# Second ConvGLU mixer in seven products: where and when the sums of its weights are loaded, and which banks its accumulators use

## The chip, the cores and the metric

One core of one Trainium2 chip runs the whole program. Its engines work side by side, each through its own list of instructions in order: TensorE (PE; PEld is its weight load), VectorE (DVE), ScalarE (ACT), GpSimd (POOL) and SyncE (SP), which here only issues DMA transfers. POOL issues transfers too: those that add what they bring to what lies at the destination ("accumulating" below). The metric is the time of one execution in device microseconds; lower is better.

## The reference, cut to what matters

A small diffusion backbone of two layers, 512 latent and 256 context tokens of width 1024, all in fp32. Layer 0 mixes tokens by attention, layer 1 by a bidirectional mLSTM. After each comes a mixer over channels, and the one of layer 1 is what is changed. It sees the 512 latent tokens only:

```
def conv_ffn(h, w_up, conv_w, conv_b, w_down):
    gate, val = jnp.split(jnp.dot(h, w_up), 2, axis=-1)      # h 512 x 1024, w_up 1024 x 5632
    return jnp.dot(jax.nn.silu(dwconv(gate, conv_w, conv_b)) * val, w_down)   # w_down 2816 x 1024
```

`dwconv` is a convolution of width 3 over tokens, per channel.

## The kernel before, in words

*The seven products.* The 2816 channels are walked in NF = 22 chunks of 128. For a chunk f the up projection is a 2 x 2 block product: two column blocks of weights (g for the gate, v for the value), each in two halves of the inner dimension (k 0 to 3, k 4 to 7), times two token halves of 256. The kernel computes it as Winograd's form of Strassen's scheme, with seven block products in place of eight. The token sides (B11, B21, B22, T1 to T4) are made once by `norm_seven`, which also does the norm. The weight sides are g itself (tile a, products 1 and 2), sums of halves of g and v (products 5, 6, 3 and 7), and the second half of v (tile d, product 4).

Every fp32 operand is split in a high part, rounded to TensorE's fp32r, and a low part, the rest: an ACT cast (L43) and a DVE subtract (L44) in `split`. A product of two operands is three matmuls, so one of the seven is 4 x 3 = 12 matmuls of 256 columns (L390).

*The sums.* They are made by DMA. `load(f)` (L404 to L415) issues, per chunk, from SP: tile a (L408, 512 KB), three plain copies of 256 KB into blocks 0, 1 and 2 of tile R (L411) and tile d (L413); and from POOL two accumulating transfers: v's first half into blocks 0 to 2 (L414), then g's first half into block 1 (L415). Block 3 is made by DVE from block 1 and the second half of a (L451, in p3). Blocks 0 and 1 are then split as "S12" for products 5 and 6, blocks 2 and 3 as "S34" for products 3 and 7. R and d have two buffers each.

*The loop.* Iteration f calls load(f+1), p1(f), p7(f-1), a down step, p2(f), p5(f), p6(f), p4(f-1), a down step, p3(f). A down step (L479 on) is one of eight output blocks of the down projection of a group of four chunks: 12 matmuls of 512 columns (L493) and a DVE addition into X (L495). Down steps begin in iteration 5. After p3 comes the convolution (L457 to L459), Silu (L461), and after p4 the products with the value half (L473, L474) and a split.

*Accumulators.* PSUM has eight banks of 512 fp32 per partition. Tag "S" gives two tiles of two banks each (`A`), and T, U, R, O are one bank each (`B`). Y takes product 1, then 6, then 7, then 4; between them u2 (L446) and v2 (L467) are read from the partial sum. Z takes product 2, and W product 5, then 3. Two chunks' Y share a tile of tag S, one bank each, so four Y exist. Z and W of a chunk are the two halves of one bank, T or U in turn; ACT copies Z out at L432 and W at L440.

*Around it.* Before the mixer stand the last part of the mLSTM (`odd`), the last two heads' share of the output projection (L1669), and `norm_seven` in two token halves. Tile R lies in pool "ffn1", which is opened after the norm, in places of "o1" (those two heads' inputs) and "nrm" before it.

*What sets the order.* The program is written in the order of these calls, but a planner (the Tile framework's) places each engine's instructions: it keeps a clock of its own for every instruction, and on an engine that is free it takes, of those that it holds for ready, the one that stands first in the program. An instruction can so come to stand far ahead of its place in the program; on the chip the engine then waits at it. A buffer is given to its next tile when the instructions that read the old one are over.

Of the kernel before, what the change touches and what calls it, by code (L numbers as in the profile page):

```python
# [32 lines left out]
class Kernel:  # L33
# [331 lines left out]
            nc.scalar.copy(B["T4"][0][:, a], g[:, b])  # L365
            low("T4", a, g[:, b], nc.vector)

    def ffn_seven(self, l, X, B, pool):

        nc, i = self.nc, self.i
        nt, n = NL, NL // 2
        cw, cb = self.fcw[l], self.fcb[l]  # L380
        neg = pool.tile([128, KD], F32, name="neg")
        nc.vector.tensor_scalar(neg, self.mod[l][:, 40:48, 0], -1.0, None, op0=MUL)
        ch, act = {}, {}
        ypair = None

        def prod(ps, w, x, first, last):
            m = 0
            for k in range(4):
                for a, b in ((w[0], x[0]), (w[1], x[0]), (w[0], x[1])):
                    nc.tensor.matmul(ps, a[:, k], b[:, k], start=first and m == 0, stop=last and m == 11,  # L390
                                     skip_group_check=True)
                    m += 1

        def pair(src, cols=KD):
            if cols == KD:
                hi, lo = self.wtile("wh", KD, 128, F32R), self.wtile("wl", KD, 128, F32R)
            else:
                hi, lo = [pool.tile([128, 4, 128], F32R, tag="d" + x, name="d" + x, bufs=1) for x in "hl"]
            self.split(hi, lo, src)
            return hi, lo  # L400

        part = lambda w, h: [x[:, 4 * h:4 * h + 4] for x in w]

        def load(f):  # L404
            c = ch[f] = {}
            g, v = i["wup"][l, f, 0], i["wup"][l, f, 1]
            c["a"] = self.wtile("wr", KD, 128, F32)
            nc.sync.dma_start(c["a"], g)  # L408
            R = c["R"] = pool.tile([128, 4, 4, 128], F32, tag="R", name="R", bufs=2)
            for j, src in enumerate((v[:, 4:8], v[:, 4:8], g[:, 0:4])):  # L410
                nc.sync.dma_start(R[:, j], src)  # L411
            c["d"] = pool.tile([128, 4, 128], F32, tag="d", name="d", bufs=2)
            nc.sync.dma_start(c["d"], v[:, 4:8])  # L413
            nc.gpsimd.dma_start(R[:, 0:3], v[:, 0:4].unsqueeze(1).to_broadcast([128, 3, 4, 128]), accum_op=ADD)  # L414
            nc.gpsimd.dma_start(R[:, 1], g[:, 0:4], accum_op=ADD)  # L415

        def p1(f):
            nonlocal ypair
            c = ch[f]
            if f % 2 == 0:  # L420
                ypair = self.A("Y")
            c["Y"] = ypair[:, 512 * (f % 2):512 * (f % 2) + n]
            c["A1"] = pair(c["a"])
            prod(c["Y"], part(c["A1"], 0), B["B11"], True, False)

        def p2(f):
            c = ch[f]
            zw = self.B("TU")
            c["W"], Z = zw[:, n:2 * n], zw[:, 0:n]
            prod(Z, part(c["A1"], 1), B["B21"], True, True)  # L430
            g = c["g"] = pool.tile([128, nt], F32, tag="g", name="g", bufs=2)
            nc.scalar.copy(g[:, 0:n], Z)  # L432
            nc.vector.tensor_tensor(g[:, 0:n], g[:, 0:n], c["Y"], op=ADD)

        def p5(f):
            c = ch[f]
            c["S12"] = pair(c["R"][:, 0:2].rearrange("p s k c -> p (s k) c"))
            prod(c["W"], part(c["S12"], 0), B["T1"], True, False)
            p = c["p5"] = pool.tile([128, n], F32, tag="p5", name="p5", bufs=2)
            nc.scalar.copy(p, c["W"])  # L440

        def p6(f):
            c = ch[f]
            prod(c["Y"], part(c["S12"], 1), B["T2"], False, False)
            u = c["u2"] = pool.tile([128, n], F32, tag="u2", name="u2", bufs=2)
            nc.scalar.copy(u, c["Y"])  # L446

        def p3(f):
            c = ch[f]
            R = c["R"]  # L450
            nc.vector.tensor_tensor(R[:, 3], R[:, 1], c["a"][:, 4:8], op=ADD)  # L451
            c["S34"] = pair(R[:, 2:4].rearrange("p s k c -> p (s k) c"))
            prod(c["W"], part(c["S34"], 1), B["B22"], False, True)
            g = c["g"]
            nc.vector.tensor_tensor(g[:, n:nt], c["u2"], c["W"], op=ADD)
            y = c["y"] = pool.tile([128, nt], F32, tag="y", name="y", bufs=2)
            nc.scalar.activation(y, g, AF.Identity, bias=cb[:, f:f + 1], scale=cw[:, 1, f:f + 1])  # L457
            nc.vector.scalar_tensor_tensor(y[:, 1:nt], g[:, 0:nt - 1], cw[:, 0, f:f + 1], y[:, 1:nt], op0=MUL, op1=ADD)
            nc.vector.scalar_tensor_tensor(y[:, 0:nt - 1], g[:, 1:nt], cw[:, 2, f:f + 1], y[:, 0:nt - 1],  # L459
                                           op0=MUL, op1=ADD)  # L460
            nc.scalar.activation(y, y, AF.Silu)  # L461

        def p7(f):
            c = ch[f]
            prod(c["Y"], part(c["S34"], 0), B["T3"], False, False)
            v = c["v2"] = pool.tile([128, n], F32, tag="v2", name="v2", bufs=2)
            nc.vector.tensor_tensor(v, c["p5"], c["Y"], op=ADD)  # L467

        def p4(f):
            c = ch[f]  # L470
            prod(c["Y"], pair(c["d"], 4), B["T4"], False, True)
            y = c["y"]
            nc.vector.tensor_tensor(y[:, 0:n], y[:, 0:n], c["Y"], op=MUL)  # L473
            nc.vector.tensor_tensor(y[:, n:nt], y[:, n:nt], c["v2"], op=MUL)  # L474
            x = act[f] = [pool.tile([128, nt], F32R, tag="a" + e, name="a" + e, bufs=8) for e in "hl"]
            self.split(*x, y)
            del ch[f]

        def down(fs):  # L479

            nf = len(fs)
            cols = min(512, 1024 // nf)
            for o in range(KD):
                if o * 128 % cols == 0:
                    w = self.weights(i["wdn"][l, fs[0]:fs[0] + nf, :, o * 128:o * 128 + cols].rearrange("f p c -> p f c"),
                                     nf, cols)
                off = o * 128 % cols
                ps = self.B("RO")
                m = 0
                for j, f in enumerate(fs):  # L490
                    wh, wl = w[j]
                    for x, y in ((wh, act[f][0]), (wl, act[f][0]), (wh, act[f][1])):
                        nc.tensor.matmul(ps, x[:, off:off + 128], y, start=m == 0, stop=m == 3 * nf - 1)  # L493
                        m += 1
                nc.vector.scalar_tensor_tensor(X[:, o], ps, neg[:, o:o + 1], X[:, o], op0=MUL, op1=ADD)  # L495
                if fs[-1] == NF - 1:
                    nc.sync.dma_start(self.out[:, o], X[:, o])
                yield

        groups = [list(range(f, min(f + 4, NF))) for f in range(0, NF, 4)]  # L500
        todo = []

        def go():
            while todo:
                if next(todo[0], 0) is None:
                    return
                todo.pop(0)

        load(0)
        for f in range(NF + 1):  # L510
            for fs in groups:
                if f == fs[-1] + 2:
                    todo.append(down(fs))
            if f + 1 < NF:
                load(f + 1)
            one, two = f < NF, f > 0
            if one:
                p1(f)
            if two:
                p7(f - 1)  # L520
            go()
            if one:
                p2(f)
                p5(f)
                p6(f)
            if two:
                p4(f - 1)
            go()
            if one:
                p3(f)  # L530
        todo.append(down(groups[-1]))
        while todo:
            go()


    def conv(self, y, ps, w, b, segs):
# [986 lines left out]
    def build(self):  # L1523
        tc, nc, i = self.tc, self.nc, self.i
        with ExitStack() as es:
# [130 lines left out]
                "p (j k t) -> p j k t", j=6, k=4)  # L1656
            B.update({nm: [z[:, 2 * j], z[:, 2 * j + 1]] for j, nm in enumerate(("T1", "T2", "T3"))})
            kept = {}
            with tc.tile_pool(name="o1", bufs=1, reuse_waits="tile") as OP, \
                    tc.tile_pool(name="nrm", bufs=1, reuse_waits="tile", side="right") as NP:  # L1660
                x = [post(h, OP, "RO") for h in (6, 7)]
                for half in range(2):
                    t = slice(256 * half, 256 * half + 256)
                    for o in range(KD):
# [6 lines left out]
                                m += 1  # L1671
                        self.xupd(1, 16, X, ps, o, 256 * half, 256, 0)
                    self.norm_seven(NP, X, 1, B, half, 256, kept)
            RP.release()


            with tc.tile_pool(name="ffn1", bufs=1, reuse_waits="tile") as FP:
                self.we = FP
                self.ffn_seven(1, X, B, FP)
                self.we = None  # L1680
            hp.release()
            HP.release()

# [103 lines left out]
```

## Time and profile before

| | us |
|---|---|
| median of 3 runs | 1864.92 (1861.98 to 1868.36) |
| profiled execution | 1872.47 |
| its span | 1870.6 |

| engine | busy us | share of the span |
|---|---|---|
| PE | 1698.6 | 91% |
| PEld | 1483.5 | 79% |
| DVE | 1332.0 | 71% |
| ACT | 811.5 | 43% |
| POOL | 314.0 | 17% |

The span runs from the first instruction to the last. Busy shares are means over stages with different limits; the second mixer is the last quarter of the span, from about 1380 us. In the chain of waits each piece is put down to what released the next one; "issue" is time for which the profile shows no releaser. In the tables of instructions, `R<-in_wup` means that tile R is written from the up weights.

### The profile page before, as it was taken

To read this page: it belongs to the slowest core of one execution; us is meant where nothing else is said; L and a number is where in the kernel's file an instruction comes from. 1 tells how busy PE (TensorE), PEld (TensorE's weight loads), DVE (VectorE), ACT (ScalarE), POOL (GpSimd) and SP (SyncE) were. 2 spreads that over 40 slices of the span, in tenths; PEclk is the share of its full clock that TensorE was granted. 3 is DMA by queue.
4 is the path that set the end of the run, shared out by engine and by line. 5 is a ranking of instruction groups with operands and counts; after the bars stand their busy time and mean duration, and the time that the engine had idled before them with its cause. 6 is when DMAs were issued, how large, how long until landed. Compare 5 with 4: busy or idle time off the path is not lost.

```text
span 1870.6 us, 27080 instructions
## 1 busy us (share of the span) xinstructions
PE 1698.6 (91%) x10222; PEld 1483.5 (79%) x10222; DVE 1332.0 (71%) x2475; ACT 811.5 (43%) x1514; POOL 314.0 (17%) x348
## 2 busy tenths in 40 slices
PE   7998899999999999999999899999955788888889
PEld 3787788888888888888888788888845787777777
DVE  7998989987875767767665777877884554555555
ACT  3337879882521312222232665555353343333332
POOL 0343554540200000000000311211041111001000
PEclk9999999999999999999999999999877898989889
DMA  8450000034343433444323411111227766555642
GB/s 295 130 160 15 11 7 18 1 137 145 114 157 102 147 113 124 136 124 136 102 91 102 125 57 46 46 57 55 93 72 171 180 158 159 139 147 152 154 109 82
DMA packets 94922, 204.15 MB, mean 109 GB/s; under 512 B 10052, under 2 KB 38724, under 8 KB 94408
## 3 DMA queue, kind: packets, MB, share of 16 engines
q1 hardware_dynamic: 82820, 179.34, 29.2%
q0 software_dynamic: 11968, 23.07, 7.3%
q8 instruction: 81, 1.33, 0.3%
q14 instruction: 49, 0.40, 0.1%
q10 hardware_dynamic: 4, 0.01, 0.0%
HBM read 198.19 MB, written 4.20 MB: 108 GB/s over the span
## 4 chain that ended last, share of the span: by engine, by line
PE 53%; DVE 17%; DMA 13%; issue 9%; ACT 7%; POOL 2%; SPq 0%; POOLq 0%; DVEq 0%; ACTq 0%
PE psS L88 18%; DMA R<-in_wup 12%; PE psU L88 4%; PE psT L588 3%; PE psU L588 3%; DVE wl L44 2%; PE psR L88 2%; PE psT L88 2%; DVE junk L141 2%; PE S L681 1%; PE psO L588 1%; PE psR L588 1%; PE psO L726 1%; PE psO L493 1%; PE psR L98 1%
## 5 line engine op out<-in xcount | busy, mean ns | idle before, releaser
L43 ACT CAST wh<-wr 128x1024 fp32r<-128x1024 f32 (+2 forms) x165 | 170.4, 1034 | 218.9 <-PE psO L588 113.0
L44 DVE TENSOR_TENSOR wl<-wr,wh 128x1024 fp32r<-128x1024 f32 (+2 forms) x165 | 201.1, 1219 | 36.9 <-ACT wh L43 34.7
L88 PE MATMUL psS<-hl,wh 128*128 128x512 f32 (+1 forms) x640 | 216.6, 339 | 1.1 <-POOL hl L297 1.1
L88 PE MATMUL psS<-hh,wh 128*128 128x512 f32 (+1 forms) x640 | 216.5, 339 | 0.4 <-ACT hh L293 0.4
L88 PE MATMUL psS<-hh,wl 128*128 128x512 f32 (+1 forms) x640 | 216.0, 338 | 0.0
L141 DVE CUSTOM_DVE_ANT_0 y<-ar,cb 128x1024 f32<-128x1024 f32 x112 | 136.4, 1218 | 0.4 <-DMA ar<-in_ada 0.4
L88 PEld LDWEIGHTS psS<-hl,wh 128*128 128x128 f32 x640 | 120.5, 188 | 16.4 <-POOL hl L297 2.1
L88 PEld LDWEIGHTS psS<-hh,wh 128*128 128x128 f32 x640 | 120.4, 188 | 15.1 <-ACT hh L293 0.9
L88 PEld LDWEIGHTS psS<-hh,wl 128*128 128x128 f32 x640 | 120.2, 188 | 14.4
L276 POOL TENSOR_TENSOR sa<-sa,sq 128x512 f32<-128x512 f32 (+1 forms) x12 | 13.5, 1124 | 590.2 <-ACT sq L275 590.2
L451 DVE TENSOR_TENSOR R<-R,wr 128x512 f32<-128x512 f32 x22 | 15.2, 691 | 126.9 <-issue 104.5
L692 POOL TENSOR_SCALAR p<-p,rs 128x768 f32<-128x768 f32 (+1 forms) x96 | 74.2, 780 | 113.4 <-DVE rs L691 70.0
L390 PE MATMUL Y<-Ts,wh 128*128 128x256 f32 x352 | 82.7, 316 | 8.4 <-DVE y L473 7.1
L141 DVE CUSTOM_DVE_ANT_0 junk<-ar,cb 128x1024 f32<-128x1024 f32 x64 | 82.0, 1281 | 0.4
L539 ACT ACTIVATE y<-psS,fcb,fcw 128x512 f32<-128x512 f32 (+1 forms) x40 | 24.7, 668 | 127.9 <-PE psS L88 127.9
L541 DVE SCALAR_TENSOR_TENSOR y<-psS,fcw,y 128x511 f32<-128x511 f32 (+1 forms) x40 | 24.5, 611 | 74.5 <-ACT y L539 74.5
L44 DVE TENSOR_TENSOR wl<-R,wh 128x1024 fp32r<-128x1024 f32 x44 | 53.7, 1221 | 33.0 <-ACT wh L43 32.9
L390 PEld LDWEIGHTS Y<-Ts,wh 128*128 128x128 f32 x352 | 68.6, 226 | 9.7 <-DVE y L473 7.3
L43 ACT CAST wh<-R 128x1024 fp32r<-128x1024 f32 x44 | 46.0, 1050 | 46.6 <-issue 19.2
L414 POOL DMA_DIRECT2D R<-in_wup x22 | 28.7, 1324 | 214.0 <-DMA R<-in_wup 190.9
L635 DVE SCALAR_TENSOR_TENSOR X<-psU,mod,X 128x512 f32<-128x512 f32 (+1 forms) x45 | 30.0, 666 | 45.9 <-PE psU L588 35.9
L684 DVE TENSOR_REDUCE nm<-S 128x1 f32<-128x768 f32 x64 | 60.1, 945 | 2.0 <-PE S L681 1.6
(791 smaller groups left out, 5578.9 us busy)
## 6 DMA issues: line engine op xcount, KB each, us to landing
ar<-in_ada SPq DMA_DIRECT2D x88, 512.0 KB, 3.7
wr<-in_wup SPq DMA_DIRECT2D x66, 512.0 KB, 3.8
wr<-in_wdn SPq DMA_DIRECT2D x44, 512.0 KB, 3.5
R<-in_wup SPq DMA_DIRECT2D x66, 256.0 KB, 3.5
R<-in_wup POOLq DMA_DIRECT2D x22, 768.0 KB, 7.3
d<-in_wup SPq DMA_DIRECT2D x22, 256.0 KB, 4.4
R<-in_wup POOLq DMA_DIRECT2D x22, 256.0 KB, 4.5
pr<-in_adak SPq DMA_DIRECT2D x8, 512.0 KB, 5.9
```

The lines of the kernel that those rows point to most:

```text
L43: nc.scalar.copy(hi, src)
L44: nc.vector.tensor_tensor(lo, src, f32(hi), op=SUB)
L88: nc.tensor.matmul(ps, a, b[:, k, x0:x0 + n], start=i == 0, stop=i == 3 * nk - 1)
L141: nc.vector.tensor_tensor_reduce(out, raw, self.cb[:, c], 1.0, 0.0, MUL, ADD, self.mraw[l][:, n, c:c + 1])
L390: nc.tensor.matmul(ps, a[:, k], b[:, k], start=first and m == 0, stop=last and m == 11, skip_group_check=True)
L414: nc.gpsimd.dma_start(R[:, 0:3], v[:, 0:4].unsqueeze(1).to_broadcast([128, 3, 4, 128]), accum_op=ADD)
L539: nc.scalar.activation(y[:, t0:t0 + n], p, AF.Identity, bias=b, scale=w[1])
L541: nc.vector.scalar_tensor_tensor(y[:, t0 + 1:t0 + n], p[:, 0:n - 1], w[0], y[:, t0 + 1:t0 + n], op0=MUL, op1=ADD)
L588: nc.tensor.matmul(ps[:, 0:n], x[:, off:off + 128], y[:, t0:t0 + n], start=m == 0, stop=m == 3 * len(fs) - 1)
L635: self.nc.vector.scalar_tensor_tensor(X[:, o, t0:t0 + n], ps[:, 0:n], self.mod[l][:, g0 + o, c:c + 1], X[:, o, t0:t0 + n], op0=MUL, op1=ADD)
L684: nc.vector.tensor_reduce(nm, s[:, 0:nk], axis=AX.X, op=MAX, negate=True)
L692: nc.gpsimd.tensor_scalar(p[:, 0:nk], p[:, 0:nk], r, 1.0, op0=MUL, op1=MUL)
```

## The change

Tile R becomes two tiles of two blocks, R12 and R34, in a pool "sums" of their own, which is opened before the output projection's last part. `load_sums(l, f)` issues their loads: two plain copies of v's second half (256 KB each) into R12, one accumulating transfer of v's first half into both blocks (512 KB), a plain copy of all of g (512 KB) into R34, g's first half accumulated into R12's second block (256 KB), v's first half accumulated into R34's first block (256 KB), and d. It is called for chunks 0 and 1 before the output projection, and for f+2 at the end of iteration f. `load(f)` loads tile a alone. The add of block 3 (before L451) moves to p5, after the split of S12, and reads R12's second block in place of tile a. p1 and p2 of chunks 0 and 1 are called ahead of the loop.

Y is now the first half of one bank, T or U in turn, so two Y exist; Z and W are a bank each of a tile of tag S. Pool "m1" (OT and other mLSTM tiles) is released before "nrm" is opened.

```diff
@@ ffn_seven
         def load(f):
-            c = ch[f] = {}
-            g, v = i["wup"][l, f, 0], i["wup"][l, f, 1]
+            c = ch[f]
             c["a"] = self.wtile("wr", KD, 128, F32)
-            nc.sync.dma_start(c["a"], g)
-            R = c["R"] = pool.tile([128, 4, 4, 128], F32, tag="R", name="R", bufs=2)
-            for j, src in enumerate((v[:, 4:8], v[:, 4:8], g[:, 0:4])):
-                nc.sync.dma_start(R[:, j], src)
-            c["d"] = pool.tile([128, 4, 128], F32, tag="d", name="d", bufs=2)
-            nc.sync.dma_start(c["d"], v[:, 4:8])
-            nc.gpsimd.dma_start(R[:, 0:3], v[:, 0:4].unsqueeze(1).to_broadcast([128, 3, 4, 128]), accum_op=ADD)
-            nc.gpsimd.dma_start(R[:, 1], g[:, 0:4], accum_op=ADD)
+            nc.sync.dma_start(c["a"], i["wup"][l, f, 0])

         def p1(f):
-            nonlocal ypair
             c = ch[f]
-            if f % 2 == 0:
-                ypair = self.A("Y")
-            c["Y"] = ypair[:, 512 * (f % 2):512 * (f % 2) + n]
+            c["Y"] = self.B("TU")[:, 0:n]
...
         def p2(f):
             c = ch[f]
-            zw = self.B("TU")
-            c["W"], Z = zw[:, n:2 * n], zw[:, 0:n]
+            zw = self.A("ZW")
+            c["W"], Z = zw[:, 512:512 + n], zw[:, 0:n]
...
         def p5(f):
-            c["S12"] = pair(c["R"][:, 0:2].rearrange("p s k c -> p (s k) c"))
+            c["S12"] = pair(c["R12"].rearrange("p s k c -> p (s k) c"))
+            nc.vector.tensor_tensor(c["R34"][:, 1], c["R34"][:, 1], c["R12"][:, 1], op=ADD)
...
         def p3(f):
-            R = c["R"]
-            nc.vector.tensor_tensor(R[:, 3], R[:, 1], c["a"][:, 4:8], op=ADD)
-            c["S34"] = pair(R[:, 2:4].rearrange("p s k c -> p (s k) c"))
+            c["S34"] = pair(c["R34"].rearrange("p s k c -> p (s k) c"))
...
         load(0)
+        load(1)
+        for f in (0, 1):
+            p1(f)
+            p2(f)
         for f in range(NF + 1):
...
-            if f + 1 < NF:
+            if 0 < f < NF - 1:
                 load(f + 1)
             one, two = f < NF, f > 0
-            if one:
+            if one and f > 1:
                 p1(f)
             if two:
                 p7(f - 1)
             go()
+            if one and f > 1:
+                p2(f)
             if one:
-                p2(f)
                 p5(f)
                 p6(f)
...
             if one:
                 p3(f)
+            if f + 2 < NF:
+                self.load_sums(l, f + 2, ch)
...
+    def load_sums(self, l, f, ch):
+        nc, pool = self.nc, self.sums
+        g, v = self.i["wup"][l, f, 0], self.i["wup"][l, f, 1]
+        c = ch[f] = {}
+        r12 = c["R12"] = pool.tile([128, 2, 4, 128], F32, tag="R12", name="R12", bufs=2)
+        r34 = c["R34"] = pool.tile([128, 2, 4, 128], F32, tag="R34", name="R34", bufs=2)
+        for j in range(2):
+            nc.sync.dma_start(r12[:, j], v[:, 4:8])
+        nc.gpsimd.dma_start(r12, v[:, 0:4].unsqueeze(1).to_broadcast([128, 2, 4, 128]), accum_op=ADD)
+        nc.sync.dma_start(r34.rearrange("p s k c -> p (s k) c"), g)
+        nc.gpsimd.dma_start(r12[:, 1], g[:, 0:4], accum_op=ADD)
+        nc.gpsimd.dma_start(r34[:, 0], v[:, 0:4], accum_op=ADD)
+        c["d"] = pool.tile([128, 4, 128], F32, tag="d", name="d", bufs=2)
+        nc.sync.dma_start(c["d"], v[:, 4:8])
@@ build
-            with tc.tile_pool(name="o1", bufs=1, reuse_waits="tile") as OP, \
-                    tc.tile_pool(name="nrm", bufs=1, reuse_waits="tile", side="right") as NP:
-                x = [post(h, OP, "RO") for h in (6, 7)]
+            self.sums = tc.alloc_tile_pool(name="sums", bufs=1, reuse_waits="tile")
+            ch = {}
+            for f in range(2):
+                self.load_sums(1, f, ch)
+            OP = tc.alloc_tile_pool(name="o1", bufs=1, reuse_waits="tile")
+            x = [post(h, OP, "RO") for h in (6, 7)]
+            RP.release()
+            with tc.tile_pool(name="nrm", bufs=1, reuse_waits="tile", side="right") as NP:
...
-            RP.release()
+            OP.release()
```

## Rows read from the trace of the kernel before

**Rows 1.** The chain that ended last, of the whole span, by engine and line.

```profile
PE psS L88 18%; DMA R<-in_wup 12%; PE psU L88 4%; PE psT L588 3%; PE psU L588 3%; DVE wl L44 2%; PE psR L88 2%; PE psT L88 2%; DVE junk L141 2%; PE S L681 1%; PE psO L588 1%; PE psR L588 1%; PE psO L726 1%; PE psO L493 1%; PE psR L98 1%
```

**Rows 2.** Busy us by stage: PE, PEld, DVE, ACT, POOL; granted clock, DMA share, GB/s.

```profile
1380.00:1400.00 20.00, 4.34 (x30) 4.12 (x28) 17.82 (x34) 11.14 (x25) 12.08 (x8) 0.67 0.08 20
...
1440.00:1500.00 60.00, 46.60 (x322) 43.93 (x321) 34.29 (x52) 24.63 (x39) 8.70 (x8) 0.89 0.73 177
1500.00:1600.00 100.00, 84.26 (x520) 76.95 (x519) 52.77 (x77) 35.36 (x52) 9.61 (x9) 0.90 0.60 152
```

**Rows 3.** The chain in time order, one period and a sum before: start, us, what.

```profile
1558.72 8.80 DMA R<-in_wup
...
1572.19 0.69 DVE R L451
...
1576.67 3.52 DMA R<-in_wup
...
1580.77 6.63 DMA R<-in_wup
1587.40 4.98 issue
```

**Rows 4.** DVE's timeline in that period: start, us, line, operation, idle before.

```profile
1574.58 1.22 DVE L44 TENSOR_TENSOR wl<-R,wh 128x1024 fp32r<-128x1024 f32 x1
...
1581.42 1.22 DVE L44 TENSOR_TENSOR wl<-R,wh 128x1024 fp32r<-128x1024 f32 x1 [3.17 <-ACT wh L43]
...
1592.38 0.69 DVE L451 TENSOR_TENSOR R<-R,wr 128x512 f32<-128x512 f32 x1 [5.95 <-issue]
...
1594.65 1.22 DVE L44 TENSOR_TENSOR wl<-R,wh 128x1024 fp32r<-128x1024 f32 x1
```

**Rows 5.** Tile R, line 451: count, ns min/median/max, first and last start.

```profile
L451 DVE TENSOR_TENSOR R<-R,wr x22: 683/691/694, 1411.0 to 1806.6; 128x512 f32<-128x512 f32 x22
```

**Rows 6.** SP's timeline in that period.

```profile
1575.82 1.28 SPq L411 DMA_DIRECT2D R<-in_wup  x3
```

**Rows 7.** POOL's timeline in that period.

```profile
1580.77 1.28 POOL L414 DMA_DIRECT2D R<-in_wup  x1 [12.06 <-DMA R<-in_wup]
1587.69 0.90 POOL L415 DMA_DIRECT2D R<-in_wup  x1 [5.64 <-DMA R<-in_wup]
```

**Rows 8.** The chain near the end: a down step and the last product 3.

```profile
1816.43 2.80 PE psO L493 x12
...
1834.81 1.42 PE psU L390 x12
```

**Rows 9.** PE's timeline where product 1 of chunk 5 starts.

```profile
1484.65 0.28 PE L390 MATMUL Y<-B11h,wh 128*128 128x256 f32 x1
```

**Rows 10.** DMA from 1500 to 1800: queues, and one load with its landing.

```profile
q1 hardware_dynamic: 17616, 29.63, 29.8%
q0 software_dynamic: 7778, 15.01, 29.5%
...
wr<-in_wup SPq DMA_DIRECT2D x14, 512.0 KB, 4.2
```

**Rows 11.** Who waited for whom, 1500 to 1800: us in total, times, longest.

```profile
PE Y L390 <- DVE v L467: 25.9, 7, 5.3
...
PE psU L390 <- ACT g L432: 17.5, 7, 3.2
```

**Rows 12.** POOL's timeline around the norm.

```profile
1361.23 1.14 POOL L318 TENSOR_TENSOR sa<-sa,sq 128x256 f32<-128x256 f32 x1 [38.33 <-ACT sq L317]
...
1397.08 2.80 POOL L414 DMA_DIRECT2D R<-in_wup  x2
```

**Rows 13.** PE's timeline: the last matmul that reads V.

```profile
1340.07 0.27 PE L1478 MATMUL num<-V,Dh 128*128 128x130 f32 x1
```

**Rows 14.** DVE's timeline: the last gate, and T2's second low part.

```profile
1353.93 0.68 DVE L1520 SCALAR_TENSOR_TENSOR OT<-gt,psT 128x512 f32<-128x512 f32 x1
...
1398.81 0.68 DVE L359 SCALAR_TENSOR_TENSOR Ts<-h,Ts 128x512 fp32r<-128x512 f32 x1
```

More of the change, by code (lines that the diff above doesn't have):

```diff
@@ L366, in norm_seven, with ffn_seven @@
             low("T4", a, g[:, b], nc.vector)
-    def ffn_seven(self, l, X, B, pool):
+    def ffn_seven(self, l, X, B, pool, ch):
         nc, i = self.nc, self.i
@@ L382, in ffn_seven @@
         nc.vector.tensor_scalar(neg, self.mod[l][:, 40:48, 0], -1.0, None, op0=MUL)
-        ch, act = {}, {}
-        ypair = None
+        act = {}
         def prod(ps, w, x, first, last):
@@ L1673, in build @@
                     self.norm_seven(NP, X, 1, B, half, 256, kept)
-            RP.release()
+            OP.release()
             with tc.tile_pool(name="ffn1", bufs=1, reuse_waits="tile") as FP:
                 self.we = FP
-                self.ffn_seven(1, X, B, FP)
+                self.ffn_seven(1, X, B, FP, ch)
                 self.we = None
+            self.sums.release()
             hp.release()
```

## The prediction

> **What bounds the kernel now.** I read the chain of waits first. Loads into tile R have 12% of it, more than any line but the biggest of TensorE's [rows 1], and R exists in the second FFN alone. The table by stage says the same: TensorE is busy for 4.3 of 20 us from 1380, for 46.6 of 60 from 1440, and from 1500 on for a steady 84 of 100 at a granted clock of 0.90 [rows 2]. So the last 490 us have two troubles: a poor start (1380 to 1500) and a steady state that TensorE doesn't set.
>
> The chain of the steady state repeats one period [rows 3]: L451 at 1572.19, plain load of R, first accumulating load, a wait of 4.98 called "issue", and L451 again at 1592.38 [rows 4]. That is 20.2 us; all 22 calls lie between 1411.0 and 1806.6 [rows 5], 18.8 apart in the mean, as the first ones, with no down projection beside them, come faster.
>
> Why is R, with two buffers, loaded once per period in a closed loop? The DVE's order shows it [rows 4]. Of the two low splits of R in a period, the one at 1574.58 is S34 of chunk c, the one at 1581.42 is S12 of chunk c+1. L451 of chunk c+2 stands on DVE at 1592.38, AHEAD of S34 of chunk c+1 (1594.65). SP issues R's loads at 1575.82, at the end of the split at 1574.58 [rows 6]: S34 of c frees the buffer for c+2. POOL issues the accumulating loads at 1580.77 and 1587.69 [rows 7], and L451 waits for the last. So the loop is: S34(c), plain load, sum, sum, L451(c+2), a few DVE instructions, S34(c+1). The planner believed L451 would be ready; it isn't, DVE stands still for 5.95 us, and the two buffers work as one. In pieces: 5.0 (1575.82 to 1580.77), 6.9 (to 1587.69), 4.7 (to 1592.38), 3.5 (to the end of the split, 1595.9).
>
> TensorE's own work per chunk is seven products of 1.42 us and two down steps of 2.80 [rows 8]: 15.5 us. The distance is 20.7: product 1 of chunk 5 starts at 1484.65 [rows 9], the last product 3 ends at 1836.23, 17 chunks later, 351.6/17. After it the queue of TensorE is full to the end at 1870.6: a tail of 34.4 us. So span = T5 + 17P + 34.4, with T5 the start of chunk 5 (1484.65) and P the period.
>
> **The change, part by part.**
>
> *Sums two chunks ahead, in two tiles.* L451 becomes an equal DVE add (512 elements, 0.69 us) inside p5, on R34[1] and R12[1]. It still stands behind a chain of loads, now gated by R12: two plain copies of v, a broadcast sum into both, the sum of g. R34's plain load (now 512 KB, which lands in about 4.2 like the other 512 KB load, [rows 10]) and its sum run beside it; only S34 needs that sum. The R12 chain: one issue of 0.43 less than now, 5.0 to 4.5. The broadcast sum into two blocks isn't in the trace: three blocks take 6.9, one takes 4.7; I take the middle, 5.8. Then 4.7. Together 15.0, then the add 0.7 and the low split 1.2: 16.9. R12 comes free with S12's split and the add, earlier than S34.
>
> Now the order. L451's place says that the planner holds three loads in a row for done within a period of the split that frees the buffer. R12(c+2) loads from S12(c) on, so by the same belief its add is ready before S12(c+1); R34's plain load begins at S34(c), 6.8 us ahead of S12(c+1) [rows 4], and one load takes 4.2, so it doesn't hold the add back. Nothing else does, and DVE takes it when it is free: ahead of S12(c+1). Then the loop closes again, S12(c), three loads, add(c+2), S12(c+1), at 16.9 plus what stands between add and split (L451 has 1.6 us between it and its split; I take the half, 0.8): P = 17.7. If the planner puts the add behind S12(c+1), the loop spans two chunks (8.5 each) and TensorE binds: 15.5 plus some residue, 16.2. Bounds for P: 15.5 from below, today's 20.7 from above, unless something new comes in.
>
> *DMA.* Per chunk 2304 KB plainly (now 2048) and 1024 KB accumulated as now. Over 1500 to 1800 with 14 chunks the queues take 29.8% and 29.5% [rows 10]: 6.4 and 6.3 us per chunk. With the 256 KB more it is 7.2 + 6.3 = 13.5: 76% at P = 17.7, 87% at 15.5. It fits, but loads will stretch: that is the reason why I don't go below 16.2.
>
> The Trainium skill, DMA: Bandwidth & Descriptors, section Anatomy of one DMA — SWDGE (gpsimd) path, prices such a transfer at 2.0 us plus bytes over 436e3: 3.2 for the two blocks and 2.6 for one. By that rule the chain would be 4.5 + 3.2 + 2.6 = 10.3 in place of 15.0, TensorE would bind, and the time would be the first rival's. The trace doesn't agree: three blocks, 3.8 by the rule, take 6.9 here [rows 7], and one takes 4.7 against 2.6 [rows 4, 7].
>
> *Accumulators.* Now Z and W share a bank, and p5 waits for ACT's copy of Z: 17.5 us over 300 in one of the two banks; p4 waits for DVE's v2, 25.9 [rows 11]. Both are mostly the standing DVE seen from TensorE (the copy L432 sits behind L461 on ACT, which waits for DVE behind L451). Own banks remove the first; that is worth nothing while the load loop binds, and up to 1.2 us per chunk where TensorE binds. In return Y has two banks instead of four: p1(f) must wait for L473 of chunk f-2. Queued behind it on TensorE is the whole next chunk; but between p4 and p1 stand a down step and p3, 4.2 us, against 0.4 for L473. Cover gone (DVE standing more than 4 us there), each us more is one of P.
>
> *The start.* The first accumulating loads now stand on POOL behind the norm's low parts and go out at 1397.08 [rows 12]; they land in series to 1411, and p5(0) starts then. The new pool lies where the heads' values V and the gates lay: V is read last at 1340 [rows 13], the last gate at 1353.93 [rows 14]. So most plain loads can go from 1341, and those over that gate from 1355. POOL is idle until 1361.23 [rows 12], so five of the six accumulating loads are issued before the norm uses it; the last may push the norm by 0 to 5 us. I take 0, as its plain load is down at about 1359. p5(0) is then bound by T1, p6(0) by T2, whose second half ends at 1399.5 [rows 14]. From there TensorE has 27.5 products to chunk 5's start (p1 and p2 of chunks 0 and 1 are done): 39 us, T5 = 1439. If chunks 2, 3 and 4 each wait for a loop of 17.7 it is 1462. I take 1450, which is 35 earlier than now.
>
> Moved with it: the splits of the first sums come into the norm's time (0.7 + 2 x 1.2 on DVE, which has 2.2 us of 20 free there, [rows 2]): 0 to 3 us, inside T5's bounds. p1 and p2 of both first chunks run there already. SP issues as many loads per chunk as now (5), and the load of d still waits for the split of the d two chunks back.
>
> **Sum.** 1450 + 17 x 17.7 + 34.4 = 1785.3, against the span of 1870.6: -85. The profiled execution took 1872.47, 7.5 above the median of 1864.92; I take the difference over to the median: 1780.
>
> **Rivals.**
> 1. TensorE binds: P = 16.2, T5 = 1440: 1749.8, -121, 1744. For it: 15.5 us of work, DVE with 52.8 busy of 100 at P = 20.7, so about 11 per chunk [rows 2], ACT less. Against it: L451's place in the order, and a DMA share of 84%.
> 2. Only the start gains: contention by the added plain loads (three blocks took 6.6 and 8.8 us in the chain, [rows 3]) and more DVE work between add and split hold P at 20; T5 = 1460: 1834.4, -36, 1829. For it: the loop keeps its form. Against it: its chain is shorter, by a smaller sum and a load less.
> 3. Slower: the three accumulating loads of a chunk come one after the other into the loop. POOL issues in order; if the planner sets R34's sum, which waits for S34(c), ahead of R12's second sum, the chain is 4.5 + 5.8 + 4.7 + 4.7 + 3.5 = 23.2 + 0.7 of waiting for R34's plain load: P = 23.9, T5 = 1465: 1905.7, +35, 1900. It is slower from P = 22.1 on (at that T5). Against it: R34's plain load is issued behind R12's.
> 4. The prefetch doesn't happen: the planner leaves the first sums behind the norm and the loop at 20.7: no change, 1865.
>
> **Chances.** Forecast 0.50, first rival 0.28, second 0.15, third 0.05, fourth 0.02. The forecast's own range is P from 17.0 to 18.7 with T5 from 1440 to 1462: 1758 to 1809. For 8 in 10 I reach down to the first rival and up to the second: 1740 to 1830. About 0.3% (6 us) is what a measurement here can tell from no change. Faster 0.93, within 0.02, slower 0.05.
>
> **What would show it.** The first p5 before 1401 and product 1 of chunk 5 at about 1450; the add on DVE ahead of S12 of the chunk before, with some 3 us of idle time; P of 17 to 19; plain queue about 7 us per chunk; no wait of p5 for L432. Wrong if TensorE is busy over 95% from 1500 on (then the first rival), if the add follows S12 in the order, if POOL holds up the norm, or if the accumulating loads stand in series.

## The result, and the profile after

The changed kernel takes 1833.01 us (median; 1831.33 to 1835.54) against 1866.64 of the kernel before, run beside it: a ratio of 0.9825 [0.9802, 0.9848], 34 us less, where 85 less were forecast. The profiled execution has a span of 1830.8, and the formula of the prediction takes the miss apart. TensorE at product 1 of chunk 5 (its timeline), and at the last product 3 (the chain):

```profile
1486.48 0.58 PE L389 MATMUL psU<-B11h,wh 128*128 128x256 f32 x1 [4.47 <-DVE y L460]
```

```profile
1793.75 1.42 PE ZW L389 x12
```

The second ends at 1795.17, and the tail after it is 35.6. So T5 = 1486.5, P = (1795.17 - 1486.48)/17 = 18.16, and against the forecast of 1785.3 for the span the start is late by 36.5, the period by 17 x 0.46 = 7.8, the tail by 1.2. The kernel before had 1484.65 and 20.7: the gain came from the period alone, and from the start nothing. Of the 36.5, 2.6 lie ahead of the output projection, whose start varies from 1356.62 to 1362.84 between the profiled runs. The 4.47 us that product 1 waits there come from DVE: L460, which reads the bank it needs, stands behind an addition (L426) that waits 7.42 us for loads:

```profile
1485.40 0.69 DVE L426 TENSOR_TENSOR R<-R,R 128x512 f32<-128x512 f32 x1 [7.42 <-issue]
```

The chain of the whole span by line, and TensorE by stage (columns as in [rows 2]):

```profile
PE psS L88 18%; DMA R<-in_wup 10%; PE psU L88 4%; PE psT L598 3%; PE psU L598 3%; DVE wl L44 2%; PE psR L88 2%; PE psT L88 2%; DVE junk L141 2%; PE ZW L389 2%; PE psR L480 2%; PE psO L480 2%; PE psO L736 1%; PE S L691 1%; PE psO L598 1%
```

```profile
1380.00:1400.00 20.00, 12.06 (x61) 11.13 (x61) 14.57 (x44) 10.68 (x25) 6.45 (x8) 0.66 0.40 96
1440.00:1500.00 60.00, 47.97 (x326) 46.45 (x327) 36.07 (x55) 25.68 (x39) 10.99 (x11) 0.82 0.76 186
1500.00:1600.00 100.00, 89.69 (x598) 80.27 (x597) 60.61 (x88) 40.98 (x61) 15.67 (x16) 1.00 0.76 188
```

Tile R still has 10% of the chain, after 12% [rows 1]. From 1500 TensorE is busy for 89.7 of 100, after 84.3; from 1440 to 1500 hardly more than before [rows 2]. The 7.7 us more from 1380 to 1400 are work that TensorE had done by then before: the output projection now runs until 1387.7.

**The loop has the form that was forecast.** DVE's order in one period, and the chain's pieces from that split on (start, us):

```profile
1613.86 1.22 DVE L44 TENSOR_TENSOR wl<-R,wh 128x1024 fp32r<-128x1024 f32 x1
...
1631.44 0.69 DVE L426 TENSOR_TENSOR R<-R,R 128x512 f32<-128x512 f32 x1 [6.44 <-DMA R<-in_wup]
...
1632.38 1.22 DVE L44 TENSOR_TENSOR wl<-R,wh 128x1024 fp32r<-128x1024 f32 x1
```

```profile
1615.10 0.33 SPq L537
...
1615.48 3.06 DMA R<-in_wup
...
1619.11 6.20 DMA R<-in_wup
1625.31 0.29 issue
1625.60 5.65 DMA R<-in_wup
```

The split at 1613.86 is S12 of chunk c, that at 1632.38 is S12 of c+1 (the S34 split between them, at 1621.07, is left out). The addition L426 of chunk c+2 stands ahead of the second and keeps DVE idle for 6.44 us until its loads are in: [rows 4] had 5.95 for L451. The waits from 1500 to 1800 put 92 us of DVE's idle time on it (columns: us in total, times, longest):

```profile
DVE R L426 <- DMA R<-in_wup: 92.2, 15, 7.2
```

Of the queues, the plain one rose from 29.8% [rows 10] to 39.8% and the accumulating one from 29.5% to 36.2%. This is read from 1500 to 1700, as the last load of sums is issued at 1758 here. At 200/18.16 = 11.0 chunks it is 7.2 and 6.6 us a chunk, where I had 7.2 and 6.3. Below the queues stand loads into R from 1500 to 1800 (POOLq: accumulating, SPq: plain), with KB each and median us to landing:

```profile
q1 hardware_dynamic: 13597, 25.49, 39.8%
q0 software_dynamic: 6095, 11.42, 36.2%
```

```profile
R<-in_wup POOLq DMA_DIRECT2D x29, 256.0 KB, 4.8
R<-in_wup SPq DMA_DIRECT2D x28, 256.0 KB, 2.6
R<-in_wup POOLq DMA_DIRECT2D x14, 512.0 KB, 6.8
```

**The start gained nothing.** The sums are loaded early, but their additions and the loads themselves got in the norm's way. DVE, POOL and the transposes of the norm's gains (L329; first and last start):

```profile
1374.44 1.04 DVE L426 TENSOR_TENSOR R<-R,R 128x512 f32<-128x512 f32 x1 [7.36 <-DMA R<-in_wup]
...
1384.12 0.69 DVE L426 TENSOR_TENSOR R<-R,R 128x512 f32<-128x512 f32 x1 [3.81 <-issue]
```

```profile
1360.39 1.38 POOL L538 DMA_DIRECT2D R<-in_wup  x1 [34.88 <-DMA R<-in_wup]
1362.57 0.89 POOL L541 DMA_DIRECT2D R<-in_wup  x1 [0.81 <-DMA R<-in_wup]
1363.78 0.73 POOL L318 TENSOR_TENSOR sa<-sa,sq 128x256 f32<-128x256 f32 x1 [0.31 <-ACT sq L317]
1370.35 0.87 POOL L540 DMA_DIRECT2D R<-in_wup  x1 [5.83 <-DMA R<-in_wup]
...
1372.22 2.71 POOL L318 TENSOR_TENSOR sa<-sa,sq 128x256 f32<-128x256 f32 x2
```

```profile
L329 PE MATMUL psO<-ident,nwy x4: 270/346/454, 1391.8 to 1401.0; 128*128 128x128 f32 x4
```

DVE stands still for 7.36 and 3.81 us among the additions of the output projection, which free its banks. POOL waits 5.83 us for the broadcast sum to land, and two sums of squares of the norm (L318) queue behind. The projection starts at 1360.29 here and at 1357.70 before, so from now on such times are counted from that start. The last transpose comes at 40.7 (before: 1383.7, which is 26.0): the norm is 14.7 us late. And since the split of S12(0) stands behind the norm's end on DVE, the buffer for chunk 2 comes free only then (DVE, then SP):

```profile
1417.52 1.22 DVE L44 TENSOR_TENSOR wl<-R,wh 128x1024 fp32r<-128x1024 f32 x1
```

```profile
1418.81 2.15 SPq L537 DMA_DIRECT2D R<-in_wup  x3
```

### The profile page after: what moved, and what is told of

The parts are those of the page before. It is cut to its first block, busy times and chain, and to the rows that moved or that the text cites. A ratio compares the mean times of both kernels' runs of the same rounds, so it can differ in the third digit from the quotient of the medians.

```text
span 1830.8 us, 27149 instructions
## 1 busy us (share of the span) xinstructions
PE 1682.3 (92%) x10222; PEld 1465.4 (80%) x10222; DVE 1332.6 (73%) x2475; ACT 811.0 (44%) x1514; POOL 330.0 (18%) x370
## 4 chain that ended last, share of the span: by engine, by line
PE 58%; DVE 17%; DMA 11%; ACT 7%; issue 5%; POOL 1%; SPq 0%; DVEq 0%; ACTq 0%; POOLq 0%
PE psS L88 18%; DMA R<-in_wup 10%; PE psU L88 4%; PE psT L598 3%; PE psU L598 3%; DVE wl L44 2%; PE psR L88 2%; PE psT L88 2%; DVE junk L141 2%; PE ZW L389 2%; PE psR L480 2%; PE psO L480 2%; PE psO L736 1%; PE S L691 1%; PE psO L598 1%
## 5 line engine op out<-in xcount | busy, mean ns | idle before, releaser
L426 DVE TENSOR_TENSOR R<-R,R 128x512 f32<-128x512 f32 x22 | 15.6, 708 | 127.2 <-DMA R<-in_wup 115.9
L551 DVE SCALAR_TENSOR_TENSOR y<-psS,fcw,y 128x511 f32<-128x511 f32 (+1 forms) x40 | 24.5, 612 | 74.5 <-ACT y L549 74.5
L43 ACT CAST ah<-y 128x768 fp32r<-128x768 f32 (+1 forms) x44 | 32.1, 729 | 73.7 <-DVE y L460 68.2
L645 DVE SCALAR_TENSOR_TENSOR X<-psU,mod,X 128x512 f32<-128x512 f32 (+1 forms) x45 | 30.0, 666 | 46.5 <-PE psU L598 37.1
L699 ACT ACTIVATE p<-S,nm 128x768 f32<-128x768 f32 x64 | 57.8, 907 | 3.8 <-DVE mvk L1056 1.3
```

Of the source, the lines that this page charges most:

```text
L43: nc.scalar.copy(hi, src)
L645: self.nc.vector.scalar_tensor_tensor(X[:, o, t0:t0 + n], ps[:, 0:n], self.mod[l][:, g0 + o, c:c + 1], X[:, o, t0:t0 + n], op0=MUL, op1=ADD)
L699: nc.scalar.activation(p[:, 0:nk], s[:, 0:nk], AF.Exp, bias=nm, accum_out=su)
```

## Experiments

Two theories for the loop: *order* (an addition waiting for loads ahead of work that is ready holds DVE) and *transfer* (the loads take a period, wherever the addition stands). For the start: the additions on DVE, POOL's order, or the late loads of chunk 2.

**Runs 1 to 3: the addition behind data that comes late.** It takes a column of ones made from a tile that must be there first: T4's low part for chunks 0 and 1 (run 1), the chunk's own S12 low split from chunk 2 on (run 2), both (run 3).

```diff
-            nc.vector.tensor_tensor(c["R34"][:, 1], c["R34"][:, 1], c["R12"][:, 1], op=ADD)
+            src = B["T4"][1][:, 3, 0:1] if f < 2 else c["S12"][1][:, 0, 0:1]
+            one = self.sm.tile([128, 1], F32, tag="one", name="one", bufs=2)
+            nc.vector.tensor_scalar(one, f32(src), 0.0, 1.0, op0=MUL, op1=ADD)
+            nc.vector.scalar_tensor_tensor(c["R34"][:, 1], c["R12"][:, 1], one, c["R34"][:, 1], op0=MUL, op1=ADD)
```

> The adds of chunks 0 and 1 are made to wait for the norm's last low part (T4), so DVE can't meet them among the output projection's additions. ORDER theory (DVE standing at the two adds, 7.4 and 3.8 us, is what holds up the norm): the norm ends some 15 us earlier, chunk 5 starts at about 1470 in place of 1486, P stays at 18.2; time 1818 (1812 to 1822). TRANSFER rival (the accumulating loads on POOL between the norm's sums, and the loads' traffic, hold it up): no change, 1833 (1829 to 1836).

> From chunk 2 on each add waits for the low split of S12 of its own chunk, so it can't stand ahead of S12 of the chunk before; the start is as in the changed kernel. ORDER theory: the loop spans two chunks, TensorE binds, P falls from 18.2 to about 16.2 and TensorE is over 95% busy from 1500 on; time 1800 (1790 to 1806). TRANSFER rival (three loads in a row plus 13.5 us of traffic per chunk bind, wherever the add stands): P stays above 17.5, time 1825 to 1835.

> Both gates together. ORDER theory: the two gains add, -15 and -33: 1785 (1775 to 1792). If the start's delay is hidden behind the first chunks' loads (chunk 2's loads go out only when the norm is over), the start gate gives less than 5 beside the loop gate: 1795 to 1800. TRANSFER rival: 1825 to 1835.

Run 1: 1830.8, ratio 0.9798 [0.9771, 0.9825]. It overlaps the changed kernel's: the additions at the start are worth some 2 us, if that, where 15 were expected. The last transpose comes at 35.1 in place of 40.7, yet the rest of the delay stays, and chunks 2 to 4 run at the loop's pace. Run 2: 1782.0, 0.9544 [0.9518, 0.9569], faster than was expected. Its DVE order over one period, and TensorE:

```profile
1600.25 1.23 DVE L44 TENSOR_TENSOR wl<-R,wh 128x1024 fp32r<-128x1024 f32 x1
...
1603.32 0.74 DVE L430 SCALAR_TENSOR_TENSOR R<-R,one,R 128x512 f32<-128x512 f32 x1
...
1616.04 1.23 DVE L44 TENSOR_TENSOR wl<-R,wh 128x1024 fp32r<-128x1024 f32 x1
```

```profile
1500.00:1600.00 100.00, 100.00 (x691) 92.08 (x690) 70.62 (x105) 47.80 (x71) 19.14 (x19) 1.00 0.87 219
```

The addition (L430) waits for nothing, TensorE is busy all the time, and the period is 15.8. DMA stands at 0.87 and holds nothing back: order, not transfer. Run 3: 1779.2, 0.9529 [0.9507, 0.9552] at P = 15.8; T5 is 115.2 after the projection's start, as in run 2 (115.5), so with the loop mended the start's additions cost next to nothing. The time of run 3 lies in the range that was given for it by chance: gains of 15 and 33 were to add up, and they were 3 and 51. POOL and the transposes in run 3:

```profile
1368.83 0.87 POOL L546 DMA_DIRECT2D R<-in_wup  x1 [7.36 <-DMA R<-in_wup]
...
1370.71 2.72 POOL L318 TENSOR_TENSOR sa<-sa,sq 128x256 f32<-128x256 f32 x2
```

```profile
L329 PE MATMUL psO<-ident,nwy x4: 272/283/323, 1382.8 to 1394.4; 128*128 128x128 f32 x4
```

The norm is still 11 us late (37.1 against 26.0), now, by this trace, behind POOL; run 7 tests that.

**Run 4: a third buffer for both sums tiles**, nothing else.

```diff
-        r12 = c["R12"] = pool.tile([128, 2, 4, 128], F32, tag="R12", name="R12", bufs=2)
-        r34 = c["R34"] = pool.tile([128, 2, 4, 128], F32, tag="R34", name="R34", bufs=2)
+        r12 = c["R12"] = pool.tile([128, 2, 4, 128], F32, tag="R12", name="R12", bufs=3)
+        r34 = c["R34"] = pool.tile([128, 2, 4, 128], F32, tag="R34", name="R34", bufs=3)
```

> The changed kernel with three buffers for R12 and R34 in place of two, nothing else. ORDER theory: the planner puts the add one chunk further ahead, again before S12 of the chunk before, and the loop of one chunk stays: P 18 to 18.6, and one more add in the norm: 1833 to 1840. BUFFER rival (two buffers are too few for three loads in a row): P falls to 16.2 and the time to about 1800.

1835.6, 0.9829 [0.9806, 0.9851]: nothing. The planner sets the addition one chunk further ahead, and DVE waits as before. Counted in DVE's order, the one below is that of chunk 15, ahead of S12 of chunk 13; in the changed kernel that of chunk 14 stands there.

```profile
1635.45 0.69 DVE L426 TENSOR_TENSOR R<-R,R 128x512 f32<-128x512 f32 x1 [7.23 <-DMA R<-in_wup]
```

**Runs 5 and 6: two parts on the kernel before.** Run 5 gates L451 of the kernel before behind its chunk's S12; run 6 gives it the new accumulators alone.

```diff
-            nc.vector.tensor_tensor(R[:, 3], R[:, 1], c["a"][:, 4:8], op=ADD)
+            one = self.sm.tile([128, 1], F32, tag="one", name="one", bufs=2)
+            nc.vector.tensor_scalar(one, f32(c["S12"][1][:, 0, 0:1]), 0.0, 1.0, op0=MUL, op1=ADD)
+            nc.vector.scalar_tensor_tensor(R[:, 3], R[:, 1], one, c["a"][:, 4:8], op0=MUL, op1=ADD)
```

```diff
-            c["Y"] = ypair[:, 512 * (f % 2):512 * (f % 2) + n]
+            c["Y"] = self.B("TU")[:, 0:n]
...
-            zw = self.B("TU")
-            c["W"], Z = zw[:, n:2 * n], zw[:, 0:n]
+            zw = self.A("ZW")
+            c["W"], Z = zw[:, 512:512 + n], zw[:, 0:n]
```

> The kernel before, with one edit: its vector addition of the fourth sum (L451) takes a tile of ones that is made from the low split of the same chunk's S12, so that it can't stand ahead of that split in the vector engine's order. No prefetch, no second tile, old accumulators. Theory (order: what bounded the loop before was that addition, waiting for a transfer of the next chunk ahead of splits whose data was there): period 20.3 -> 15.8 to 16.5, time 1785 to 1800. Rival (the two pools' transfers are too slow for one period and need the two tiles): period 18.5 to 20, time 1835 to 1867.

> The kernel before, with the changed kernel's accumulators alone (Y in a bank of its own, Z and W in the two banks of a pair). Theory (the loop over loads binds, TensorE waits anyway): the time stays within 0.3%, 1861 to 1871. Rival (TensorE's waits for banks are on the path): up to 1.2 us a chunk, 1840 to 1850.

Run 5: 1794.6, 0.9604 [0.9586, 0.9622], 74 us less from three lines, and 38 below the changed kernel, without a prefetch or a second tile. TensorE from 1500 to 1700; from 1600 on it is busy all the time here too:

```profile
1500.00:1600.00 100.00, 95.16 (x635) 86.38 (x634) 72.38 (x108) 48.94 (x70) 13.06 (x12) 0.97 0.77 193
1600.00:1700.00 100.00, 100.00 (x687) 91.71 (x686) 73.84 (x111) 48.51 (x69) 13.98 (x13) 1.00 0.80 207
```

Run 6: 1870.7, 1.0016 [1.0002, 1.0029]: if anything 0.2% slower, within the bound of 0.3%.

**Runs 7, 9, 11 and 12: POOL's order in the start.** Run 7 is run 3 with all 14 POOL operations of the second norm on VectorE, run 9 the same on run 5, which has no prefetch. Run 11 moves in run 3 only the six sums of squares, run 12 in run 5 only the four low parts of B22 and T3.

```diff
-                (nc.vector if k % 2 else nc.gpsimd).tensor_tensor(sa[k % 2], sa[k % 2], sq, op=ADD)
+                nc.vector.tensor_tensor(sa[k % 2], sa[k % 2], sq, op=ADD)
...
-                low(nm, kk, h[:, k], nc.gpsimd if k % 2 else nc.vector)
+                low(nm, kk, h[:, k], nc.vector)
...
-            low("B22", a, h[:, b], nc.gpsimd)
+            low("B22", a, h[:, b], nc.vector)
...
-            low("T3", a, h[:, a], nc.gpsimd)
+            low("T3", a, h[:, a], nc.vector)
```

> The changed kernel with both gates (as the run before of that kind, 1779), and all 14 GpSimd operations of the second norm given to VectorE. Theory (in that run the norm is late since GpSimd's second summing load waits for the first to land, 7.4 us, ahead of the norm's sum of squares in GpSimd's order): the norm's second transposes come 6 to 10 us earlier (1391 -> 1381 to 1385), and the time falls by 4 to 9: 1770 to 1775. Rival 1 (load traffic slows the output projection and the norm, not the order on GpSimd): 1778 to 1781. Rival 2 (VectorE's some 7 us of added work stand on the path): 1782 to 1787.

> The kernel before with the gated addition (as the run that took 1794.6), and all 14 GpSimd operations of the second norm given to VectorE, as in the run at 1769.8. A control: there is no load of sums on GpSimd during the norm here. Theory (the 9.4 us which that edit saved with the prefetch came from GpSimd's order, waiting loads ahead of the norm's sums): 1791 to 1798. Rival (VectorE is just the better engine for these operations): 1783 to 1787.

> The changed kernel with both gates; of the second norm's GpSimd operations only the six sums of squares (L318) go to VectorE, the eight low parts stay. Theory (in the run with both gates those sums stand in GpSimd's order behind summing loads that wait): the second transposes come as early, counted from the start of the output projection, as with all 14 moved (26.8 us, not 37.1), and most of the 9.4 us is there: 1770 to 1774. Rival (the low parts matter, not the sums): 1777 to 1780, transposes at 35 to 37.

> The kernel before with the gated addition (1794.6); of the second norm's GpSimd operations only the four low parts of B22 and T3 go to VectorE, those that stand directly ahead of the first summing loads in GpSimd's order; sums and the other low parts stay. Theory (without the prefetch it is GpSimd's order the other way: the first loads of sums wait for the norm's last operations): the first summing load goes out near 1384 in place of 1398.6, and the time is that of the run with all 14 moved: 1782 to 1787. Rival (VectorE does the norm's sums faster than GpSimd): 1791 to 1795.

Run 7: 1769.8, 0.9475 [0.9455, 0.9495], 9.4 less than run 3. The transposes:

```profile
L329 PE MATMUL psO<-ident,nwy x4: 273/284/323, 1375.0 to 1387.7; 128*128 128x128 f32 x4
```

That is 26.8 after the projection's start, 0.8 later than before the change. Run 9, the control, missed: 1784.0, 0.9538 [0.9519, 0.9557], the rival's figure. The trace gives the rival no support, though: the last transpose comes at 27.2, against 26.4 in run 5. VectorE doesn't bring the norm to that point any sooner; something else moved. POOL in run 5, then in run 9:

```profile
1397.07 1.59 POOL L333 TENSOR_TENSOR Ts<-h,Ts 128x512 fp32r<-128x512 f32 x1 [1.28 <-ACT Ts L361]
1398.61 2.80 POOL L414 DMA_DIRECT2D R<-in_wup  x2
```

```profile
1380.81 1.48 POOL L414 DMA_DIRECT2D R<-in_wup  x1 [55.40 <-DVE B11l L333]
1383.68 1.28 POOL L414 DMA_DIRECT2D R<-in_wup  x1 [1.39 <-DMA R<-in_wup]
```

Without the prefetch it is POOL's order the other way round: the first summing loads stand behind the norm's last operations, as in [rows 12]. With those operations off POOL, the first of them goes out 18 us earlier, and S12(0) is split 9 us earlier, as soon as the norm lets DVE go. In run 5 (first below) DVE waits for it, in run 9 it hardly does:

```profile
1412.99 1.23 DVE L44 TENSOR_TENSOR wl<-R,wh 128x1024 fp32r<-128x1024 f32 x1 [9.78 <-ACT wh L43]
```

```profile
1403.71 1.23 DVE L44 TENSOR_TENSOR wl<-R,wh 128x1024 fp32r<-128x1024 f32 x1 [0.26 <-ACT wh L43]
```

Runs 11 and 12 were made to tell the two directions apart; run 11 came out inside what was expected, run 12 0.3 us below it. Run 11: 1773.0, 0.9485 [0.9456, 0.9513], last transpose at 28.0: most of run 7's gain lies in the sums of squares, which stood behind waiting loads. Run 12: 1781.7, 0.9535 [0.9509, 0.9562], all of run 9's gain with the norm's sums still on POOL. Counted from the projection's start, the first summing load goes out at 24.5 (run 5: 39.8), S12(0) is split 12.4 us sooner than in run 5, and chunk 5 starts 12.1 sooner, against 12.8 us of time:

```profile
1386.59 0.76 POOL L333 TENSOR_TENSOR B21l<-h,B21h 128x256 fp32r<-128x256 f32 x1 [0.86 <-ACT B21h L342]
1387.30 2.79 POOL L414 DMA_DIRECT2D R<-in_wup  x2
```

**Runs 8 and 10: three chunks ahead, and the old accumulators on top.** Run 8 is run 7 with a third buffer and the first three chunks' sums loaded during the output projection (the load of d moves to that of tile a, which wasn't tested by itself). Run 10 is run 8 with the accumulators of the kernel before.

```diff
-            for f in range(2):
+            for f in range(3):
                 self.load_sums(1, f, ch)
...
-            if f + 2 < NF:
-                self.load_sums(l, f + 2, ch)
+            if f + 3 < NF:
+                self.load_sums(l, f + 3, ch)
```

> As the run with the norm's GpSimd work on VectorE, and a third buffer of each sums tile, with the sums three chunks ahead, the first three chunks during the output projection (the plain copy of the weights that S4 needs moves to the load of W1 to keep its two buffers). Theory (with the adds in place, what is left of the start is that chunk 2's sums are loaded only after S12(0) is split, behind the norm): p1(5) comes 8 to 15 us earlier than with two chunks, time 1757 to 1768. Rival (the norm is held by still more load traffic, or chunks 3 and 4 wait for transfers just as long): within 3 us of the run with two chunks, or slower.

> As the run with three chunks of sums ahead (1761.0), with the accumulators of the kernel before: Y in halves of a pair, Z and W in halves of one bank. Theory (where TensorE has no idle time left, its waits for banks come back: the kernel before had 1.18 us a chunk of them by its waits): 1765 to 1787, with the period up from 15.8 to 16 to 17. Rival (TensorE's order by the planner hides them): 1758 to 1764.

Run 8: 1761.0, 0.9422 [0.9401, 0.9443], 8.8 below run 7. Product 1 of chunk 5 starts at 92.0 after the projection's start (run 7: 103.6):

```profile
1450.52 0.28 PE L389 MATMUL psU<-B11h,wh 128*128 128x256 f32 x1
```

Of those 11.6 us 6.3 are given back at once, as chunk 6 starts 22.1 later (run 7: 15.8). The load of the first down weights takes 9.01 us of the chain (first line), and TensorE stands still for 3.1 us in two waits, the longer one below. The same matmuls then take 19.06 us at a granted clock of 0.85, where run 7 has 15.80 at 1.00:

```profile
1445.70 9.01 DMA wr<-in_wdn
```

```profile
1455.84 0.50 PE L488 MATMUL psR<-ah,wh 128*128 128x512 f32 x1 [2.30 <-ACT wh L43]
```

```profile
1450.52:1472.64 22.12, 19.06 (x111) 16.74 (x109) 13.88 (x22) 9.10 (x14) 5.99 (x6) 0.85 0.93 221
```

So 5.3 us stay. Of the 8.1 us between the two profiled executions, 2.4 lie ahead of the projection, and so within what its start varies between runs. Run 10: 1760.0, 0.9406 [0.9385, 0.9427], the same as run 8: the rival was right, also where TensorE has no idle time left:

```profile
1500.00:1600.00 100.00, 100.00 (x693) 92.02 (x692) 73.67 (x111) 48.69 (x71) 19.71 (x20) 1.00 0.86 217
```

## Why the prediction was wrong

**The step that failed is the start:** "five of the six accumulating loads are issued before the norm uses it; the last may push the norm by 0 to 5 us. I take 0", and from it T5 = 1450. T5 came at 126.2 after the projection's start; the forecast, on the execution before, was 1450 - 1357.7 = 92.3. Two of the six loads, not five, went out ahead of the norm's first sum on POOL, and the push was not 0: the last transpose came 14.7 us late, 10.3 of which POOL's order explains (37.1 in run 3, 26.8 in run 7). POOL holding up the norm was among the prediction's own signs of being wrong. Three things were wrong:
- The loads of the sums go out from 1355.37, behind the load of tile a (1354.94) in SP's order, not from 1341 (lines below). On POOL, the second sum of a chunk waits for the first to land (5.83 us), and the norm's sums queue behind that. I counted issues on POOL and left the wait inside them out. The Trainium skill, PSUM — Partial Sum Buffer, section Engine vs sequencer instructions, calls the queues of ScalarE, VectorE and GpSimd strictly first in, first out; the trace agrees, with 5.83 us here and 7.36 in run 3. Taken off POOL, the norm's operations gave 11.6 us of T5 (run 7 against run 3).
- I put the first additions into no one's way on DVE. They held it for 11.2 us among the output projection's own; it mattered little (run 1), as POOL held the same norm.
- Chunk 2's loads wait for S12(0). I had the first splits "come into the norm's time"; that of S12(0) stands behind the norm, at 1417.52, and the first p5 with it, not before 1401. For chunks 2 to 4 I took the middle between TensorE alone (1439) and a loop of 17.7 (1462). With the loop mended 10.7 us of T5 are gone (run 2 against the changed kernel), with a third chunk ahead 11.6 (run 8 against run 7).

```profile
1354.94 0.33 SPq L406 DMA_DIRECT2D wr<-in_wup  x1
1355.37 0.85 SPq L537 DMA_DIRECT2D R<-in_wup  x2
```

In the order of runs 2, 3, 7 and 8, the steps of 10.7, 0.3, 11.6 and 11.6 lead from 126.2 to 92.0. That 92.0 is the forecast T5 is chance, as the forecast counted neither on a third chunk nor on a mended loop. With two chunks ahead and POOL free of the norm, T5 comes at 103.6 (run 7). POOL's order wasn't tested with the addition ungated, as the changed kernel has it.

**The loop was right in mechanism** (the addition ahead of S12 of the chunk before, 6.4 us of idle time where I said 3) **and off in size.** From S12's split to the next it is 1.2 for the split, 4.0 from issue to the first sum, 6.5 for the broadcast sum, 5.8 for the second, 0.9 to the split: 18.5 in that period, 18.16 in the mean, where I had 17.7. The mis-sized terms are the broadcast sum (5.8 forecast, 6.5) and the last one (4.7, 5.8); the issue (4.5) and the step from add to split (1.5) were a little shorter than I took them. An estimate from the Trainium skill's fit (DMA: Bandwidth & Descriptors, section Anatomy of one DMA — SWDGE (gpsimd) path), 3.2 and 2.6 us for the two loads, is again below what the trace shows, 6.8 and 4.8 in the median. With the addition out of the way TensorE binds in spite of such loads (run 2): their order decided, not their price.

**The rest.** "If the planner puts the add behind S12(c+1) ... TensorE binds" holds, at 15.8 and not 16.2; from 1500 on, a DMA share of 0.87 in run 2 stretched no load so far that TensorE waited. Accumulators: nothing while the loop binds, as said (run 6), but also nothing beyond it (run 10), where I allowed up to 1.2 a chunk. The waits in [rows 11] were the standing DVE: in run 10, with the same accumulators and the addition gated, TensorE stands nowhere from 1500 to 1600. The second rival had nearly the measured time (1829) with its parts exchanged: it let the start gain and the loop stand still. Two slips in the sums changed nothing: 300 us are 14.5 periods of 20.7 and not 14 chunks (6.2 and 6.1 us of queue a chunk, not 6.4 and 6.3), and the third rival is slower from P = 21.8 on, not 22.1.

Where the change's gain lies: with the addition gated, prefetch, tiles and banks together give 15 us (run 5 against run 3), with the norm's POOL work moved as well 14 (run 9 against run 7). The gate gives 74 on the kernel before and 51 on the changed one. What stays open is why the planner thinks those loads done so early. The fastest version, run 10 or 8, is 5.8 to 5.9% below the kernel before and 4% below the changed one.

## What to carry to other kernels

Before buying buffers or moving loads, look for an instruction that waits for a transfer ahead of ready work on an in-order engine. Tying it to data that comes late (three lines) gave more here than the whole prefetch, and a third buffer alone gave nothing. When loads that sum are moved to GpSimd's idle time, count the wait between two of them that need one another, and what stands behind it; a control that moves the same work without the prefetch shows which direction of the queue was paid for.

## What was not expected of the hardware

An accumulating load costs more than a plain one of its size: for 256 KB into tile R 4.5 us before and 4.8 after, against 3.1 and 2.6 plain, in medians over 1500 to 1800. One of 768 KB, which adds one source to three blocks, took 6.9 before, hardly more than one of 512 KB to two blocks after (6.8). The loads of the kernel before:

```profile
R<-in_wup SPq DMA_DIRECT2D x42, 256.0 KB, 3.1
R<-in_wup POOLq DMA_DIRECT2D x14, 768.0 KB, 6.9
...
R<-in_wup POOLq DMA_DIRECT2D x14, 256.0 KB, 4.5
```

A DMA share of 0.87 at 219 GB/s left TensorE busy for 100 of 100 us in run 2, while in run 8, at 0.93 (1450 to 1473), it stood for 3.1 us on one load. The granted clock was 1.00 in run 2's stretch; it was 0.90 at 84 of 100 busy in the kernel before [rows 2] and 0.82 from 1440 to 1500 in the changed kernel, at 48 of 60.
